# Forgetting attention in eight heads: row maxima as a running fused minimum, transposed by one matmul

## The chip, the cores and the metric

The kernel runs on one core of a Trainium2 chip. The time is the device time of one execution in microseconds (us). The engines are TensorE (PE; its weight loads are PEld), VectorE (DVE), ScalarE (ACT), GpSimd (POOL) and SyncE (SP, which here only issues transfers).

## The reference

One layer over a sequence of 2048 tokens with 1024 channels. A normalised input is projected into three groups of heads: a gated linear recurrence, a pooling mixer, and a causal attention of 8 heads of 64 channels with a forgetting term. The branches are gated, concatenated and projected back. The change touches the attention alone:

```python
c = jnp.cumsum(log_f, axis=1).transpose(0, 2, 1)
scale = D ** -0.5
for i in range(T // Q_BLOCK):
    s = jnp.einsum('bqhd,bkhd->bhqk', q[:, q0:q1], k[:, :q1]).astype(jnp.float32) * scale
    mask = (q0 + jnp.arange(Q_BLOCK))[:, None] >= jnp.arange(q1)[None, :]
    bias = jnp.where(mask, c[:, :, q0:q1, None] - c[:, :, None, :q1], 0.0)
    p = jax.nn.softmax(jnp.where(mask, s + bias, MASK_VALUE), axis=-1)
    outs.append(jnp.einsum('bhqk,bkhd->bqhd', p.astype(v.dtype), v[:, :q1]))
```

So each row of scores has q·k / 8 plus c at the query minus c at the key, and the softmax needs something near the row's maximum to be subtracted before the exponential.

## The kernel before

**Up to the attention.** Until about 673 us of the profiled execution the kernel normalises and projects, runs the recurrence (the tiles S, el and pu belong to it), and writes the attention's q and k as float16 pairs (high and low part) to scratch memory (qh_d, ql_d, kh_d, kl_d). `fgates` cumulates the forget gates; it leaves the cumulated gate of each key, scaled, as two rows per head in c_d (chi and clo, with rows of 256 ahead of them), the reference value of each query group in cref8, and the bias of the exponential in biasg. The pooling mixer (tile mb among others) comes next, and then v.

**The attention.** Queries are worked on in 4 groups (g) of 512 tokens, 8 heads (h) each, so 32 pairs of group and head; keys come in chunks (c) of 512. Group g sees chunks 0 to g. For each pair there are two passes.

- `max_steps` finds the row maxima. For each block of 128 queries (qi) and each chunk, PE makes the scores `mx` (512 keys wide; in the last, diagonal chunk 128 to 512) from QM and KA. Rows 0 to 63 of these are q and k; a few rows from 64 on carry the constants and the gate (68 rows in all). DVE reduces each mx to one value per query: a plain reduction (L979) for a whole chunk, and for the diagonal one a fused operation that adds the mask negq and takes the maximum (L976, two instructions in the trace: the operation and a read of its accumulator). Then L985 takes the maximum over the chunks, L986 adds cref8 and scales, and L988 and L989 split the result in a float16 pair, Mc. Three passes later (MTL), `mt` turns Mc with four matmuls (L995), one for each 128 queries, into two rows of 512, and ACT copies them to rows 64 and 65 of QB (L997). The helper `bank` gives the PSUM tiles: three for mx, two for st, one for o and two for ty, which mt, the gate projection and the output share.
- `scores` and `values` make the attention itself: for each 128 keys (j) two matmuls fill `st` (L1009 from the high and low parts, L1010 from KA and QB, where QB's maxima meet the 256s in KA), and on the diagonal a third adds the mask (L1012). ACT takes the exponential as float32 (pf, L1019) and as float16 (ph, L1023; every third one is made by POOL, L1021), and DVE or POOL subtracts the two (pl, L1024). `values` multiplies both with v in `o` (L1034 to L1036), and after a head's last key DVE divides (rl, oc).

**Order.** A list `deadlines` spreads the passes of `max_steps` over the steps of the head before (LEAD steps ahead of their use), and generators fill the remaining room: the gate projection (pgc), the loads of the output weights (wo, wol), then the output projection (y, yt, L1078 to L1095) of groups that are done. The order in which each engine gets its instructions is then set by a scheduler, and each engine runs its own in order.

Of the kernel before, what the change touches and what calls it, by code (L numbers as in the profile page):

```python
# [54 lines left out]
def kernel(  # L55
# [33 lines left out]
    cref8 = cp.tile([P, NG, 8], F32, tag="cref8", name="cref8")  # L89
# [8 lines left out]
    c_d = tc.dram_tile([4, 8, T], F16, name="c_d")  # L98
# [611 lines left out]
    def fgates():  # L710
# [53 lines left out]
        V.tensor_scalar(c32, crs[0], -1.0 / 32, None, op0=ALU.mult)  # L764
# [4 lines left out]
        for i, src in enumerate((c256, c256, chi, clo)):  # L769
            nc.sync.dma_start(c_d[i].rearrange("h (t c) -> t h c", c=P), src)  # L770
# [21 lines left out]
    def kload(c):  # L792
        tok = ds(c * GT, GT)
        nc.sync.dma_start(KA[c][64:68], c_d[:, :, tok])
        nc.sync.dma_start(KA[c][0:64], kh_d[:, :, tok].rearrange("c (e p) t -> p (c e) t", p=64))
        nc.sync.dma_start(K2[c][0:64], kh_d[:, :, tok].rearrange("c (e p) t -> p (c e) t", p=64))
        nc.sync.dma_start(K2[c][64:128], kl_d[:, :, tok].rearrange("c (e p) t -> p (c e) t", p=64))
# [158 lines left out]
    def max_steps():  # L956
        for n, (g, h) in enumerate(order):
# [7 lines left out]
            M = wk.tile([P, 4, 4], F32, tag="M", name=f"M{g}_{h}", bufs=2) if g else None  # L965
            Mf = wk.tile([P, 4], F32, tag="Mf", name=f"Mf{g}_{h}", bufs=2)
            left = MTL if n else 0
            for qi in range(4):
                for c in range(g + 1):
# [3 lines left out]
                    PE.matmul(mx[:, :w], QMs[i][:68, qi * P:(qi + 1) * P], KA[c][:68, h, :w], start=True, stop=True)  # L973
                    dst = M[:, qi, c:c + 1] if g else Mf[:, qi:qi + 1]
                    if last:
                        V.tensor_tensor_reduce(mx[:, :w], mx[:, :w], negq[:, GT - w:], 1.0, -3e38,  # L976
                                               op0=ALU.add, op1=ALU.max, accum_out=dst)
                    else:
                        V.tensor_reduce(dst, mx[:, :w], op=ALU.max, axis=AX.X)  # L979
# [4 lines left out]
            if g > 0:  # L984
                V.tensor_reduce(Mf, M[:, :, :g + 1], op=ALU.max, axis=AX.X)  # L985
            V.tensor_scalar(Mf, Mf, cref8[:, g, h:h + 1], -1.0 / 256, op0=ALU.add, op1=ALU.mult)  # L986
            Mc = wk.tile([P, 4, 2], F16, tag="Mc", name=f"Mc{g}_{h}", bufs=2)
            V.tensor_copy(Mc[:, :, 0], Mf)  # L988
            V.tensor_tensor(Mc[:, :, 1], Mf, Mc[:, :, 0], op=ALU.subtract)  # L989
            yield n  # L990

            def mt(g=g, h=h, i=i, Mc=Mc):
                pt = bank("ty", f"mt{g}_{h}")
                for qi in range(4):
                    PE.matmul(pt[64:66, qi * P:(qi + 1) * P], Mc[:, qi, :], idh, start=qi == 0, stop=qi == 3,  # L995
                              skip_group_check=True)
                S.activation(QBs[i][64:66], pt[64:66], AF.Copy, bias=0.0, scale=1.0)  # L997
# [4 lines left out]
    def scores(n, g, h, j):  # L1002
# [7 lines left out]
        PE.matmul(st[:, off:], KA[c][:68, h, jj * P:(jj + 1) * P], QBs[i][:68, off:], start=False, stop=not diag)  # L1010
# [192 lines left out]
```

## Time and profile before

| | us |
|---|---|
| runs: median of 3 (lowest to highest) | 1248.82 (1247.80 to 1250.89) |
| the profiled execution | 1248.18 |
| its span in the profile | 1246.4 |
| PE / DVE / ACT / POOL busy | 1170.5 / 812.2 / 609.5 / 403.7 |
| first row maximum, last row maximum (matmul mx) | 673.1, 1144.4 |

A row of a group of instructions reads: line of the kernel, engine, operation, output <- inputs, shape, count, then busy time in us and the mean length of one in ns, then idle time of the engine just ahead of them and what ended it. In a row of a tile, three numbers divided by strokes are the shortest, median and longest duration in ns. Granted clock is 0.987 on average. Matmuls are pipelined: one of 512 columns is listed with 0.38 us though the next starts after 0.22.

### The profile page before, as it was taken

The page shows a single profiled execution, that of the slowest core. Times are in us where ns is not written, and L with a number is a line of the kernel's source. Part 1 is how long each engine was busy: PE and PEld are TensorE (multiplying, and loading weights), DVE is VectorE, ACT ScalarE, POOL GpSimd, SP SyncE. Part 2 cuts the span into 40 slices and gives each one's busy share as a digit, 9 for nine tenths or more (in the row PEclk, how much of TensorE's full clock was granted, in tenths as well). Part 3 has the DMA queues.
Part 4 walks back from the last instruction along what each step waited for, and adds up shares of the span by engine and source line. Part 5 has one row for each costly group of instructions (what it writes and reads, how often), then busy time and mean ns, then how long its engine had stood idle before and what let it go on. Part 6 is the DMA issues. An engine that isn't in the chain of part 4 may idle for free.

```text
span 1246.4 us, 25487 instructions
## 1 busy us (share of the span) xinstructions
PE 1170.5 (94%) x9949; PEld 749.9 (60%) x9949; DVE 812.2 (65%) x1736; ACT 609.5 (49%) x1176; POOL 403.7 (32%) x500
## 2 busy tenths in 40 slices
PE   5877999999999999999999999999989899999998
PEld 3445667655644588884447767755555555555544
DVE  5787878887433243214364799788788888888522
ACT  5756444553121222212122677667767676777611
POOL 2645555553130020002230223234334343434400
PEclk9988999999999999999999999999999999999999
DMA  9646100113175232101112343285223222321263
GB/s 226 184 115 170 44 17 18 52 35 93 43 183 142 71 107 71 35 2 43 26 51 70 89 140 110 69 178 127 67 64 85 68 78 79 65 51 38 80 162 104
DMA packets 168137, 107.56 MB, mean 86 GB/s; under 512 B 95824, under 2 KB 159568, under 8 KB 168016
## 3 DMA queue, kind: packets, MB, share of 16 engines
q1 hardware_dynamic: 166976, 105.92, 32.2%
q8 instruction: 78, 1.28, 0.4%
q14 instruction: 43, 0.35, 0.1%
q10 hardware_dynamic: 1040, 0.00, 0.0%
HBM read 59.62 MB, written 31.59 MB: 73 GB/s over the span
## 4 chain that ended last, share of the span: by engine, by line
PE 62%; DVE 19%; ACT 6%; issue 5%; POOL 4%; DMA 4%; SPq 0%; POOLq 0%; DVEq 0%; ACTq 0%
PE y L1078 11%; PE pq L183 7%; PE pv L194 6%; PE pgc L194 5%; PE pu L183 3%; PE st L1009 3%; PE st L1010 3%; PE pgb L183 3%; PE pk L183 3%; DVE pl L1024 3%; PE mx L973 3%; DVE M L979 3%; PE o L1034 2%; PE o L1035 2%; PE pf L183 2%
## 5 line engine op out<-in xcount | busy, mean ns | idle before, releaser
L1019 ACT ACTIVATE pf<-st,biasg 128x512 f32<-128x512 f32 (+1 forms) x320 | 199.6, 625 | 93.9 <-PE st L1010 53.2
L194 PEld LDWEIGHTS <-hTh 128*128 128x128 f16 x1536 | 151.0, 99 | 44.3 <-DMA hTh<-xh 16.1
L1024 DVE TENSOR_TENSOR pl<-pf,ph 128x512 f16<-128x512 f32 (+1 forms) x213 | 139.9, 658 | 42.4 <-POOL ph L1021 24.8
L1024 POOL TENSOR_TENSOR pl<-pf,ph 128x512 f16<-128x512 f32 (+2 forms) x107 | 114.2, 1067 | 147.7 <-ACT ph L1023 137.6
L979 DVE TENSOR_REDUCE M<-mx 128x1 f32<-128x512 f32 x192 | 129.2, 682 | 9.4 <-PE mx L973 8.5
L1023 ACT ACTIVATE ph<-st,biasg 128x512 f16<-128x512 f32 (+2 forms) x213 | 131.4, 617 | 2.1 <-PE o L1036 2.1
L1034 PE MATMUL o<-Vt,ph 128*128 128x65 f16 x1088 | 129.7, 193 | 2.8 <-DVE oc L1048 2.4
L1035 PE MATMUL o<-Vt,ph 128*128 128x64 f16 x1088 | 130.2, 195 | 0.0
L1036 PE MATMUL o<-Vt,pl 128*128 128x65 f16 x1088 | 129.2, 192 | 0.0
L1021 POOL TENSOR_SCALAR ph<-pf 128x512 f16<-128x512 f32 (+1 forms) x107 | 66.0, 617 | 192.4 <-ACT pf L1019 130.8
L1034 PEld LDWEIGHTS <-ph 128*128 128x128 f16 x1088 | 102.6, 96 | 34.5 <-issue 5.5
L1009 PE MATMUL st<-QQ,K 128*128 128x512 f16 (+1 forms) x320 | 111.5, 349 | 5.6 <-ACT ph L1023 5.0
L1035 PEld LDWEIGHTS <-ph 128*128 128x128 f16 x1088 | 101.8, 97 | 24.5 <-issue 1.1
L1036 PEld LDWEIGHTS <-pl 128*128 128x128 f16 x1088 | 102.3, 99 | 0.4
L1078 PE MATMUL y<-woh,mh 128*128 128x512 f16 (+2 forms) x264 | 98.2, 373 | 0.0
L1078 PE MATMUL y<-woh,ml 128*128 128x512 f16 (+2 forms) x264 | 98.0, 373 | 0.0
L1078 PE MATMUL y<-wol,mh 128*128 128x512 f16 (+2 forms) x264 | 98.0, 373 | 0.0
L973 PE MATMUL mx<-KA,QM 68*128 68x512 f16 (+1 forms) x224 | 79.5, 358 | 5.7 <-DVE M L979 4.1
L194 PEld LDWEIGHTS <-hTl 128*128 128x128 f16 x768 | 75.5, 98 | 9.9
L1010 PE MATMUL st<-QB,KA 68*128 68x512 f16 x224 | 80.1, 358 | 0.0
L1078 PEld LDWEIGHTS <-mh 128*128 128x128 f16 x528 | 49.4, 98 | 50.4 <-issue 0.7
L976 DVE CUSTOM_DVE_ANT_0 mx<-mx,negq 128x128 f32<-128x128 f32 (+3 forms) x128 | 62.3, 492 | 12.0 <-PE mx L973 11.5
(327 smaller groups left out, 2691.1 us busy)
## 6 DMA issues: line engine op xcount, KB each, us to landing
xt<-in_x_dram SPq DMA_DIRECT2D x16, 512.0 KB, 4.4
xr<-in_x_dram SPq DMA_DIRECT2D x16, 512.0 KB, 4.5
out_dram<-yt SPq DMA_DIRECT2D x15, 512.0 KB, 3.1
QQ<-qh_d SPq DMA_DIRECT2D x64, 64.0 KB, 2.3
wo<-in_w_out_dram SPq DMA_DIRECT2D x16, 256.0 KB, 3.0
gc_d<-gtc SPq DMA_DIRECT2D x32, 128.0 KB, 2.0
gtl<-gc_d SPq DMA_DIRECT2D x16, 256.0 KB, 2.9
wst_q<-in_w_in_dram SPq DMA_DIRECT2D x12, 256.0 KB, 2.9
```

The costliest lines, as they stand in the source:

```text
L183: PE.matmul(ps, a[:, k, c0:c0 + P], b[:, k, :], start=i == 0, stop=i == 3 * KC - 1)
L194: PE.matmul(ps, a[:, k, :], b[:, k, c0:c0 + n], start=i == 0, stop=i == 3 * KC - 1)
L979: V.tensor_reduce(dst, mx[:, :w], op=ALU.max, axis=AX.X)
L1009: PE.matmul(st[:, off:], K2[c][:, h, jj * P:(jj + 1) * P], QQs[i][:, off:], start=True, stop=False)
L1010: PE.matmul(st[:, off:], KA[c][:68, h, jj * P:(jj + 1) * P], QBs[i][:68, off:], start=False, stop=not diag)
L1019: S.activation(pf[:, off:], st[:, off:], AF.Exp, bias=bias, scale=0.125)
L1023: S.activation(ph[:, off:], st[:, off:], AF.Exp, bias=bias, scale=0.125)
L1024: (G if k == 1 else V).tensor_tensor(pl[:, off:], pf[:, off:], ph[:, off:], op=ALU.subtract)
L1034: PE.matmul(pov[:, qi, :], ph[:, qs], Vt[:, j, h, 0:65], start=(j == 0 and qi == 0), stop=False, skip_group_check=True)
L1035: PE.matmul(pov[:, qi, 0:64], ph[:, qs], Vt[:, j, h, 65:129], start=False, stop=False, skip_group_check=True)
L1036: PE.matmul(pov[:, qi, :], pl[:, qs], Vt[:, j, h, 0:65], start=False, stop=(j == 4 * g + qi), skip_group_check=True)
L1078: PE.matmul(py, a[:, k, :], b[:, k, cs], start=i == 0, stop=i == 3 * KC - 1)
```

## The change

It keeps a running minimum of the negated maxima. The scores of a chunk are multiplied by -1/256 in the same fused operation that reduces them, with the value after the earlier chunks as the start of the minimum, so that the value after the last chunk is the result. For this the gate rows of c_d are now relative to each group's own reference, and `gap8`, made once in `fgates`, has the distance from group to group; it is added in the fused operation as a broadcast operand where the mask stands for the diagonal chunk. The reduction over chunks and the scaling go.

The four blocks of 128 queries of Mc are transposed by one matmul into eight rows, two for each block. DVE multiplies them with `bm`, a table of ones and zeros, into rows 64 to 71 of QB, so that each block's two rows are nonzero only in its own 128 columns. ACT's copy goes. KA and QM get ten rows from 64 on instead of four.

```diff
-        G.memset(qm[64:68], 256.0)
-        G.memset(qm[64:66], 0.0)
+        G.memset(qm[64:74], 256.0)
+        G.memset(qm[64:72], 0.0)
...
+    G.memset(bm, 1.0)
+    G.affine_select(out=bm, in_=bm, pattern=[[-2, 4]], compare_op=ALU.is_ge, fill=0.0, base=-64, channel_multiplier=1)
+    G.affine_select(out=bm, in_=bm, pattern=[[2, 4]], compare_op=ALU.is_ge, fill=0.0, base=65, channel_multiplier=-1)
...
+        for g in range(NG):
+            V.tensor_tensor(gap8[:, g], cref8[:, g:g + 1, :].to_broadcast([P, NG, 8]), cref8, op=ALU.subtract)
...
-        V.tensor_scalar(c32, crs[0], -1.0 / 32, None, op0=ALU.mult)
+        for g in range(NG):
+            V.tensor_scalar(c32[32 * g:32 * g + 32], crs[g][32 * g:32 * g + 32], -1.0 / 32, None, op0=ALU.mult)
...
-        for i, src in enumerate((c256, c256, chi, clo)):
+        for i, src in enumerate((c256,) * 8 + (chi, clo)):
             nc.sync.dma_start(c_d[i].rearrange("h (t c) -> t h c", c=P), src)
...
-        nc.sync.dma_start(KA[c][64:68], c_d[:, :, tok])
+        nc.sync.dma_start(KA[c][64:74], c_d[:, :, tok])
...
-                    PE.matmul(mx[:, :w], QMs[i][:68, qi * P:(qi + 1) * P], KA[c][:68, h, :w], start=True, stop=True)
-                    dst = M[:, qi, c:c + 1] if g else Mf[:, qi:qi + 1]
-                    if last:
-                        V.tensor_tensor_reduce(mx[:, :w], mx[:, :w], negq[:, GT - w:], 1.0, -3e38,
-                                               op0=ALU.add, op1=ALU.max, accum_out=dst)
-                    else:
-                        V.tensor_reduce(dst, mx[:, :w], op=ALU.max, axis=AX.X)
+                    PE.matmul(mx[:, :w], QMs[i][:74, qi * P:(qi + 1) * P], KA[c][:74, h, :w], start=True, stop=True)
+
+                    off = negq[:, GT - w:] if last else gap8[:, g, c, h:h + 1].to_broadcast([P, w])
+                    V.tensor_tensor_reduce(mx[:, :w], mx[:, :w], off, -1.0 / 256, M[:, qi, c - 1:c] if c else 3e38,
+                                           op0=ALU.add, op1=ALU.min, accum_out=M[:, qi, c:c + 1])
...
-            if g > 0:
-                V.tensor_reduce(Mf, M[:, :, :g + 1], op=ALU.max, axis=AX.X)
-            V.tensor_scalar(Mf, Mf, cref8[:, g, h:h + 1], -1.0 / 256, op0=ALU.add, op1=ALU.mult)
             Mc = wk.tile([P, 4, 2], F16, tag="Mc", name=f"Mc{g}_{h}", bufs=2)
-            V.tensor_copy(Mc[:, :, 0], Mf)
-            V.tensor_tensor(Mc[:, :, 1], Mf, Mc[:, :, 0], op=ALU.subtract)
+            V.tensor_copy(Mc[:, :, 0], M[:, :, g])
+            V.tensor_tensor(Mc[:, :, 1], M[:, :, g], Mc[:, :, 0], op=ALU.subtract)
...
-                for qi in range(4):
-                    PE.matmul(pt[64:66, qi * P:(qi + 1) * P], Mc[:, qi, :], idh, start=qi == 0, stop=qi == 3,
-                              skip_group_check=True)
-                S.activation(QBs[i][64:66], pt[64:66], AF.Copy, bias=0.0, scale=1.0)
+                PE.matmul(pt[64:72, :P], Mc.rearrange("p q two -> p (q two)"), idh, start=True, stop=True)
+                V.tensor_tensor(QBs[i][64:72].rearrange("p (q c) -> p q c", q=4),
+                                pt[64:72, :P].unsqueeze(1).to_broadcast([8, 4, P]),
+                                bm[64:72].unsqueeze(2).to_broadcast([8, 4, P]), op=ALU.mult)
...
-        PE.matmul(st[:, off:], KA[c][:68, h, jj * P:(jj + 1) * P], QBs[i][:68, off:], start=False, stop=not diag)
+        PE.matmul(st[:, off:], KA[c][:74, h, jj * P:(jj + 1) * P], QBs[i][:74, off:], start=False, stop=not diag)
```

The order of the instructions on the engines shows what moves. In these rows mx_5_3_2 is head 5, query block 3, chunk 2, pl_4_5 is head 4, key block 5, and the last number of a name is that of its buffer; ISA is the fused operation or, with one name only, the read of its accumulator. On DVE, in group 2 at the end of head 5, before:

```order
L976 ISA mx_5_3_2_11253,M_5_10947<-mx_5_3_2_11253,negq 128x512 [waits PE_49]
L976 ISA M_5_10947 128x1
L1051 TENSOR_TENSOR oc_2_10852<-oc_2_10852,gtl_2_10853 128x512 [waits DMAHW2_49,DVE_49]
L1024 TENSOR_TENSOR pl_4_5_11234<-pf_4_5_11232,ph_4_5_11233 128x512 [waits PE_49,Activation_49]
L985 TENSOR_REDUCE Mf_5_10948<-M_5_10947 128x4 [waits DVE_49]
L1024 TENSOR_TENSOR pl_4_6_11266<-pf_4_6_11264,ph_4_6_11265 128x512 [waits PE_49,Pool_49]
L411 TENSOR_TENSOR mx_2_l<-oc_2_10852,mx_2_h 128x512 [waits Activation_49]
L986 TENSOR_SCALAR Mf_5_10948<-Mf_5_10948,cref_74 128x4 [waits DVE_49]
L979 TENSOR_REDUCE M_6_11289<-mx_6_0_0_11291 128x1 [waits PE_49]
L988 CAST Mc_5_11258<-Mf_5_10948 128x4 [waits DVE_49]
L979 TENSOR_REDUCE M_6_11289<-mx_6_0_1_11315 128x1 [waits PE_49]
L989 TENSOR_TENSOR Mc_5_11258<-Mf_5_10948,Mc_5_11258 128x4 [waits DVE_49]
```

The same place of the changed kernel, on DVE:

```order
L987 ISA mx_5_3_2_11160,M_5_10858<-mx_5_3_2_11160,negq,M_5_10858 128x512 [waits DVE_49,PE_49]
L987 ISA M_5_10858 128x1
L1057 TENSOR_TENSOR oc_2_10765<-oc_2_10765,gtl_2_10766 128x512 [waits DMAHW0_49,DVE_49]
L1030 TENSOR_TENSOR pl_4_5_11141<-pf_4_5_11139,ph_4_5_11140 128x512 [waits PE_49,Activation_49]
L994 CAST Mc_5_11163<-M_5_10858 128x4 [waits DVE_49]
L1030 TENSOR_TENSOR pl_4_6_11171<-pf_4_6_11169,ph_4_6_11170 128x512 [waits PE_49,Pool_49]
L413 TENSOR_TENSOR mx_2_l<-oc_2_10765,mx_2_h 128x512 [waits Activation_49]
L995 TENSOR_TENSOR Mc_5_11163<-M_5_10858,Mc_5_11163 128x4 [waits DVE_49]
L987 ISA mx_6_0_0_11195,M_6_11194<-mx_6_0_0_11195,gap_74 128x512 [waits PE_49]
L987 ISA M_6_11194 128x1
L987 ISA mx_6_0_1_11219,M_6_11194<-mx_6_0_1_11219,gap_74,M_6_11194 128x512 [waits DVE_49,PE_49]
L987 ISA M_6_11194 128x1
```

The last step of Mc now stands ahead of the next head's first two maxima; before, it stood behind them. The second of these maxima takes the first one's result and waits for it on its own engine (DVE_49). Of the 192 fused operations with such an input, 52 stand directly behind the read that they need. On PE, at the transposition that follows, before:

```order
L973 MATMUL mx_6_0_2_11343<-K_9289,QM_3246 128x128 [waits DVE_49]
L995 LDWEIGHTS Mc_5_11258 [waits DVE_49]
L995 MATMUL mt_5_11346<-idh,Mc_5_11258 2x128
L995 LDWEIGHTS Mc_5_11258
L995 MATMUL mt_5_11346<-idh,Mc_5_11258 2x128
L995 LDWEIGHTS Mc_5_11258
L995 MATMUL mt_5_11346<-idh,Mc_5_11258 2x128
L995 LDWEIGHTS Mc_5_11258
L995 MATMUL mt_5_11346<-idh,Mc_5_11258 2x128
L1009 LDWEIGHTS K_9289
```

On PE, the changed kernel at the same place:

```order
L984 MATMUL mx_6_0_2_11247<-K_9232,QM_3247 128x128 [waits DVE_49]
L1000 LDWEIGHTS Mc_5_11163 [waits DVE_49]
L1000 MATMUL mt_5_11250<-idh,Mc_5_11163 8x128
L1015 LDWEIGHTS K_9232
L1015 MATMUL st_4_9_11253<-QQ_3240,K_9232 128x384 [waits Activation_49]
```

mt stays where it was, behind the third maximum of the next head, with one matmul instead of four. On DVE, shortly behind, the changed kernel has the write of QB that ACT had:

```order
L987 ISA mx_6_0_2_11247,M_6_11194<-mx_6_0_2_11247,negq,M_6_11194 128x128 [waits DVE_49,PE_49]
L987 ISA M_6_11194 128x1
L1030 TENSOR_TENSOR pl_4_8_11228<-pf_4_8_11226,ph_4_8_11227 128x512 [waits Activation_49]
L1001 TENSOR_TENSOR QB_3244<-mt_5_11250,bm 8x512 [waits PE_49]
L1030 TENSOR_TENSOR pl_4_9_11259<-pf_4_9_11257,ph_4_9_11258 128x384 [waits Pool_49]
```

It stands behind the reduction of the mx that PE makes just ahead of mt, with one pl between them.

More of the change, by code (lines that the diff above doesn't have):

```diff
@@ L88 @@
     biasg = cp.tile([P, NG, P], F32, tag="biasg", name="biasg")
-    cref8 = cp.tile([P, NG, 8], F32, tag="cref8", name="cref8")
+    gap8 = cp.tile([P, NG, NG, 8], F32, tag="gap8", name="gap8")
+    bm = cp.tile([P, 4], F32, tag="bm", name="bm")
     qh_d = tc.dram_tile([4, P, T], F16, name="qh_d")
@@ L97 @@
     gc_d = tc.dram_tile([T, 512], F32, name="gc_d")
-    c_d = tc.dram_tile([4, 8, T], F16, name="c_d")
+    c_d = tc.dram_tile([10, 8, T], F16, name="c_d")
     mh_d = tc.dram_tile([T, 6 * P], F16, name="mh_d")
@@ L698 @@
         qm = vp.tile([P, GT], F16, tag=f"QM{i}", name=f"QM{i}")
-        G.memset(qm[64:68], 256.0)
-        G.memset(qm[64:66], 0.0)
+        G.memset(qm[64:74], 256.0)
+        G.memset(qm[64:72], 0.0)
         qb = vp.tile([P, GT], F16, tag=f"QB{i}", name=f"QB{i}")
-        G.memset(qb[64:68], 0.0)
+        G.memset(qb[64:74], 0.0)
         QMs.append(qm)
@@ L756, in fgates @@
         V.tensor_copy(dl, pdl[:, :NG])
+        cref8 = fp.tile([P, NG, 8], F32, tag="cref8", name="cref8")
         V.tensor_scalar(cref8.rearrange("p g h -> p (g h)"), pcr[:, :32], 8.0, None, op0=ALU.mult)
+        for g in range(NG):
+            V.tensor_tensor(gap8[:, g], cref8[:, g:g + 1, :].to_broadcast([P, NG, 8]), cref8, op=ALU.subtract)
         crs = []
@@ L964, in max_steps @@
             nc.sync.dma_start(QBs[i][0:64], ql_d[h // 2, r, tok])
-            M = wk.tile([P, 4, 4], F32, tag="M", name=f"M{g}_{h}", bufs=2) if g else None
-            Mf = wk.tile([P, 4], F32, tag="Mf", name=f"Mf{g}_{h}", bufs=2)
+            M = wk.tile([P, 4, NG], F32, tag="M", name=f"M{g}_{h}", bufs=2)
             left = MTL if n else 0
```

## The prediction

> **What bounds the kernel now.** I read the page first, then busy time by stage, then the waits, the groups and the order of time on VectorE (DVE), the engine that gets the new work. The page: the span, the two busiest engines, and the chain of waits by engine.
>
> ```profile
> span 1246.4 us, 25487 instructions
> PE 1170.5 (94%) x9949; PEld 749.9 (60%) x9949; DVE 812.2 (65%) x1736; ACT 609.5 (49%) x1176; POOL 403.7 (32%) x500
> PE 62%; DVE 19%; ACT 6%; issue 5%; POOL 4%; DMA 4%; SPq 0%; POOLq 0%; DVEq 0%; ACTq 0%
> ```
>
> TensorE (PE) is the bound over the whole, DVE comes second. The change lies in the attention, where these shares differ. The next rows are stretches: everything from 343 us up to the first row maximum, then the four query groups as the row maxima reach them (from 673.1, 716, 824 and 994 us), then the tail. Columns: stretch, length, busy time of each engine.
>
> ```profile
> core 0: us, PE busy (x) PEld busy (x) DVE busy (x) ACT busy (x) POOL busy (x), PEclk, DMA share, GB/s
> 343.00:673.00 330.00, 325.33 (x2170) 214.10 (x2169) 116.10 (x250) 75.63 (x173) 49.57 (x66) 1.00 0.27 73
> 673.10:716.00 42.90, 41.05 (x447) 31.21 (x445) 32.33 (x120) 25.20 (x53) 9.05 (x14) 0.96 0.27 77
> 716.00:824.00 108.00, 102.65 (x1228) 77.55 (x1225) 92.56 (x242) 75.59 (x149) 33.32 (x42) 1.00 0.39 107
> 824.00:994.00 170.00, 157.10 (x1793) 92.71 (x1792) 147.93 (x330) 118.89 (x218) 65.81 (x78) 1.00 0.41 100
> 994.00:1148.00 154.00, 148.50 (x1681) 86.84 (x1680) 133.59 (x275) 112.64 (x199) 62.78 (x73) 0.99 0.25 63
> ```
>
> From 673 to 1148 us, 475 us in all, DVE is busy 32.3 + 92.6 + 147.9 + 133.6 = 406 us (86%) and PE 449 us (95%, its ends modelled). DVE has some 69 us of slack, so it is not idle cover: PE and DVE are near each other. ScalarE (ACT), at 332 us (70%), has room. The chain inside this stretch, by line:
>
> ```profile
> by line: PE y L1078 13.1%; PE pgc L194 9.5%; PE st L1009 7.8%; DVE pl L1024 7.5%; PE mx L973 7.4%; PE st L1010 7.3%; DVE M L979 7.0%; PE o L1034 4.5%; PE o L1035 4.5%; PE o L1036 4.3%; issue 3.4%; DVE mx L976 2.8%; DMA wo<-in_w_out_dram 2.1
> ```
>
> The plain reductions (L979) stand on it with 7.0% of 475 us, 33 us. Their group, with the others of DVE in the same stretch:
>
> ```profile
> L1024 DVE TENSOR_TENSOR pl<-pf,ph 128x512 f16<-128x512 f32 (+1 forms) x198 | 130.6, 661 | 30.4 <-POOL ph L1021 20.6 <-ACT ph L1023 7.9
> L979 DVE TENSOR_REDUCE M<-mx 128x1 f32<-128x512 f32 x192 | 129.2, 682 | 9.4 <-PE mx L973 8.5
> L976 DVE DVE_READ_ACCUMULATOR2_ANT M<- 128x1 f32 x96 | 13.3, 139 | 0.0
> L1086 DVE TENSOR_TENSOR yt<-y,gpo 128x512 f32<-128x512 f32 x17 | 11.6, 683 | 0.6 <-ACT ojunk L1085 0.4
> L986 DVE TENSOR_SCALAR Mf<-Mf,cref 128x4 f32<-128x4 f32 x32 | 10.4, 327 | 0.3
> L985 DVE TENSOR_REDUCE Mf<-M 128x4 f32<-128x8 f32 (+2 forms) x24 | 3.8, 157 | 0.2
> ```
>
> 33 of 129.2 us: a microsecond of DVE work costs 0.26 us of time today. The subtraction pl (L1024) gives the same, 7.5% of 475 = 36 of 130.6 us, 0.27. Who waits for whom in the stretch (total, times, longest):
>
> ```profile
> ACT QB L997 <- PE mt L995: 12.8, 14, 3.8
> DVE mx L976 <- PE mx L973: 11.5, 21, 1.8
> PE mx L973 <- DVE M L979: 6.1, 8, 1.8
> PE mt L995 <- DVE Mc L989: 5.9, 7, 1.2
> PE mx L973 <- DVE M L976: 2.5, 3, 2.0
> ```
>
> PE stands 8.6 us for a bank of row scores that DVE has not reduced, and 5.9 us for Mc, the two-part maxima that the transposing matmul mt takes. DVE stands for PE as well. Two engines wait for each other in turn.
>
> **The change, part by part.** *The reduction.* 192 plain reductions become the fused operation plus a read of its accumulator; the 128 diagonal ones have that already. DVE in order of time (start, length):
>
> ```profile
> 1028.45 0.68 DVE L979 TENSOR_REDUCE M<-mx 128x1 f32<-128x512 f32 x1
> 1029.06 0.69 DVE L976 CUSTOM_DVE_ANT_0 mx<-mx,negq 128x512 f32<-128x512 f32 x1
> 1029.66 0.14 DVE L976 DVE_READ_ACCUMULATOR2_ANT M<- 128x1 f32 x1
> 1029.84 0.17 DVE L985 TENSOR_REDUCE Mf<-M 128x4 f32<-128x16 f32 x1
> ...
> 865.48 0.14 DVE L976 DVE_READ_ACCUMULATOR2_ANT M<- 128x1 f32 x1
> 865.48 0.69 DVE L1024 TENSOR_TENSOR pl<-pf,ph 128x512 f16<-128x512 f32 x1
> ```
>
> From start to start the reduction takes 0.61 us (1028.45 to 1029.06) and the fused one 0.60 (1029.06 to 1029.66). The read costs nothing where the next instruction does not need it (both at 865.48), and 0.18 us where it does (1029.66 to 1029.84). So the swap as such is nearly free. What is new is that 192 of the 320 now take the maximum so far as a per-partition operand. No such fused operation is in the trace; the nearest row with a per-partition operand beside a PSUM tensor and an SBUF tensor is mb, against 683 ns of yt, which has none:
>
> ```profile
> L867 DVE SCALAR_TENSOR_TENSOR mb<-pp,pscl,gtb x8: 742/746/750, 581.5 to 654.2; 128x512 f32<-128x512 f32 x8
> L378 DVE SCALAR_TENSOR_TENSOR S<-S,el,pu x64: 254/280/289, 74.8 to 326.6; 64x64 f32<-64x64 f32 x64
> ```
>
> 0.746 - 0.683 = 0.06 us, times 192 = 12 us. In the order of the changed kernel 52 of the 192 stand directly behind the read that they need: 52 x 0.18 = 9 us. Together 21 us of DVE; the ends are 0 (operand free, PE late anyway) and 192 x 0.24 = 46 us (each one exposed). I take 21, since mb has the operands and the order has the neighbours.
>
> *The bookkeeping.* The reduction over chunks (L985, 3.8 us) and the scaling (L986, 10.4) go: -14.2 us of DVE. The two steps that make Mc stay.
>
> *The transposition.* Four matmuls a head become one: 96 go. Around one of them:
>
> ```profile
> 929.92 0.22 PE L973 MATMUL mx<-K,QM 68*128 68x128 f16 x1
> 931.33 0.38 PE L995 MATMUL mt<-idh,Mc 128*2 128x128 f16 x4 [1.18 <-DVE Mc L989]
> ```
>
> Four take 0.38 us where one takes 0.22, so each further one starts 0.053 later: 96 x 0.053 = 5 us of PE, at most, and I count it all, PE being the chain for most of the time. This row also shows the wait. DVE, at the same place:
>
> ```profile
> 929.05 0.22 DVE L986 TENSOR_SCALAR Mf<-Mf,cref 128x4 f32<-128x4 f32 x1
> 929.19 0.68 DVE L979 TENSOR_REDUCE M<-mx 128x1 f32<-128x512 f32 x1
> 929.79 0.83 DVE L988 CAST Mc<-Mf 128x4 f16<-128x4 f32 x1
> 930.53 0.68 DVE L979 TENSOR_REDUCE M<-mx 128x1 f32<-128x512 f32 x1
> 931.13 0.15 DVE L989 TENSOR_TENSOR Mc<-Mf,Mc 128x4 f16<-128x4 f32 x1
> ```
>
> Two reductions of the next head stand between the steps. In the new order both steps of Mc stand ahead of them, some 1.2 us earlier, as long as these seven waits. But a DVE that is behind is late for something else next, a bank of mx above all: of 5.9 us I count 3 as saved, between 0 and 5.9.
>
> *The write of QB* moves from ACT to DVE:
>
> ```profile
> L997 ACT ACTIVATE QB<-mt 2x512 f16<-2x512 f32 x32 | 18.8, 588 | 14.2 <-PE mt L995 13.5
> ```
>
> On ACT it lay off the path, and I count nothing for its going. On DVE it is a product of 8 x 512 read from PSUM. By yt it takes 0.683 us; the 8 partitions save nothing, as S with 64 partitions and 64 elements takes 280 ns. 32 x 0.683 = 22 us (19 if each overlaps the next as the reductions do). Behind it in DVE's queue stand pl and the next maxima, for which PE waits. It waits for mt, as ACT did; since PE issues mt just behind the mx whose reduction stands ahead of QB, I count no stall. The consumer, the second score matmul, follows some passes later.
>
> One rule of the Trainium skill speaks against this part: VectorE: DVE Perf Modes, section "Two Vector instructions with no wait between them", says that an instruction whose operands start in another quadrant of partitions than those of the one before starts only when all earlier ones have finished. QB starts at partition 64, so it and its successor would each lose the 0.08 us by which 0.68-us operations overlap here: 64 x 0.08 = 5 us more of DVE, an estimate that by the price below makes the sum 2 us longer.
>
> *Before the attention*: six more stores of c_d, ten rows instead of four into KA, four products for gap8, four partial scalings, wider memsets. PE is busy 325.3 of 330 us there and DVE 116, so these have cover: 0, at most +1 us. The matmuls contract 74 rows instead of 68: nothing, as 68 and 128 rows take the same:
>
> ```profile
> L1009 PE MATMUL st<-QQ,K 128*128 128x512 f16 x224 | 85.1, 380 | 4.5 <-ACT ph L1023 4.1
> L1010 PE MATMUL st<-QB,KA 68*128 68x512 f16 x176 | 67.0, 381 | 0.0
> ```
>
> *The sum.* DVE: +21 + 22 - 14 = +29 us, which takes it from 406 to 435 of 475 us (86 to 92%) beside a PE that gets lighter. The price of 0.27 is that of today; as DVE's slack shrinks from 69 to 40 us, the price rises towards 1. I take 0.42, nearer the row: 29 x 0.42 = +12. PE -5, the wait for Mc -3. Together +4 us, on the profiled execution's 1248.2: 1252.2. It stands 0.6 us below the median of the runs shown (1248.82), so 1252.8, rounded 1253. Ends: DVE +29 - 21 + 3 for a free operand and shorter QB would be near +5, at 0.27 +1, with -5 and -6: -10, 1239; DVE +54 at 0.6, +32, with -5: +27, 1276.
>
> **The rivals.** About 0.3% (3.7 us) is what a measurement of this kernel can tell from no change.
>
> *Faster: DVE's load stays in its slack* (0.28). For it: 69 us of slack, of which 20 us are waits for PE's own mx, and seven waits for Mc that the order undoes. Then the exposed reads cost nothing (+12 + 19 - 14 = +17 of DVE, at 0.27 +5), PE -5, Mc -6: -6 us, 1243. It decides itself at PE's wait for mx: if that stays near 9 us, this holds. Against it: those waits come in turn, and a longer pass on DVE moves the next one.
>
> *No change* (0.29): the same 29 us at today's price, +8, against -5 and -3: 1249.
>
> *DVE becomes the bound* (0.07, within slower): with 435 us of work and the last group at 134 + 15 of 154 us, the price is near 1: +29 - 5 - 3 = +21, 1270. Against it: three banks of mx and five of pl still let the engines slip past each other.
>
> *The running maximum contends with GpSimd* (0.03, within slower): its operands in SBUF are two. L1024, with two SBUF inputs, shows such stalls:
>
> ```profile
> L1024 DVE TENSOR_TENSOR pl<-pf,ph x213: 274/681/1667, 680.4 to 1175.3; 128x512 f16<-128x512 f32 x75, 128x384 f16<-128x384 f32 x15, 128x128 f16<-128x128 f32 x9, 128x256 f16<-128x256 f32 x8
> ```
>
> Were the 192 held up by 0.1 us on average, that is +19 of DVE, +8 us: 1261. Against it stands S, with a per-partition operand and a tensor in SBUF: 254 to 289 ns, never stalled. The Trainium skill, SBUF — State Buffer, section "Who interferes with whom", has the contention for two SBUF inputs and doesn't say whether a per-partition operand is one; by S it is none.
>
> *The change doesn't do what it says* (0.01): excluded but for numbers of the schedule, since the new order shows one mt a head and the fused pairs.
>
> **How the numbers follow.** Slower 0.43 (my sum, 1253, in its own range 1250 to 1262, with the two heavier cases), same 0.29, faster 0.28. The range reaches from 1240 (faster, near its end) to 1266, leaving out DVE as a full bound and the last of the gains.
>
> **What would show it.** Fused operations with the running maximum near 0.75 us; DVE busy near 435 us from the first row maximum to the last; mt with 32 records and a wait for Mc under 3 us; QB on DVE near 0.68 us; PE's wait for mx grown from 9 towards 20 us. If that wait stays, the forecast is wrong towards faster. If QB waits long for mt, or fused operations take over 0.85 us, it is wrong towards slower.

## The result, and the profile after

| | before | after |
|---|---|---|
| median of 5 runs (lowest to highest), us | 1250.89 (1247.80 to 1251.91) | 1256.60 (1254.60 to 1258.87) |
| the profiled execution, us | 1248.18 | 1254.60 |

The ratio is 1.0052, with a 95% interval from 1.0037 to 1.0067: the change made the kernel slower by some 6 us. The prediction was 1253, with slower as its likeliest case.

The page of the changed kernel, with the same three lines as before:

```profile
span 1252.9 us, 25621 instructions
PE 1170.2 (93%) x9853; PEld 749.3 (60%) x9853; DVE 846.7 (68%) x1911; ACT 589.9 (47%) x1144; POOL 414.0 (33%) x503
PE 63%; DVE 18%; issue 6%; ACT 5%; POOL 4%; DMA 4%; SPq 0%; DVEq 0%; POOLq 0%; ACTq 0%
```

96 matmuls are gone (9949 to 9853), and still PE is listed as busy for the same time. DVE has 34.5 us more in all. The stretches again, each from a group's first row maximum to the next group's. Of before stand here the last three, since the prediction began its last group at 994 us where group 3 begins at 962.7, and the sum from the first to the last row maximum:

```profile
716.00:822.50 106.50, 101.35 (x1221) 77.01 (x1218) 91.06 (x238) 74.09 (x147) 32.57 (x41) 1.00 0.38 106
822.50:962.70 140.20, 131.03 (x1485) 76.93 (x1482) 122.07 (x277) 99.79 (x182) 55.06 (x66) 1.00 0.44 104
962.70:1144.40 181.70, 172.26 (x1968) 101.12 (x1965) 157.92 (x327) 129.81 (x232) 71.96 (x85) 0.99 0.25 64
673.10:1144.40 471.30, 445.69 (x5104) 286.27 (x5102) 403.38 (x958) 328.88 (x611) 168.65 (x204) 0.99 0.34 87
```

And of after:

```profile
343.00:672.10 329.10, 325.39 (x2171) 214.12 (x2170) 117.34 (x257) 75.63 (x173) 49.42 (x66) 1.00 0.29 75
672.10:711.70 39.60, 38.29 (x426) 29.50 (x424) 34.34 (x121) 21.51 (x46) 10.11 (x15) 1.00 0.30 83
711.70:820.30 108.60, 100.36 (x1197) 76.10 (x1194) 98.28 (x259) 68.56 (x137) 32.10 (x41) 1.00 0.37 104
820.30:967.10 146.80, 136.28 (x1463) 80.16 (x1459) 134.18 (x335) 95.29 (x174) 59.83 (x66) 0.94 0.42 100
967.10:1150.90 183.80, 172.61 (x1943) 100.56 (x1940) 168.96 (x414) 124.92 (x224) 75.11 (x86) 0.99 0.23 64
672.10:1150.90 478.80, 447.54 (x5011) 286.32 (x5009) 435.75 (x1126) 310.28 (x580) 177.16 (x205) 0.98 0.33 86
```

Until the attention nothing is lost: the first row maximum comes 1 us earlier. Group 0 is 3.3 us shorter, group 2 is 6.6 us longer, groups 1 and 3 are 2.1 us longer each, and from the first to the last row maximum it is 7.5 us. DVE is busy for 435.75 us from the first to the last row maximum, against 403.38. In group 2 the granted clock falls to 0.94. Who waits for whom in the attention (total, times, longest), and the groups of DVE:

```profile
PE o L1040 <- DVE oc L1054: 11.9, 10, 2.3
PE mx L984 <- DVE M L987: 9.4, 11, 2.2
PE mt L1000 <- DVE Mc L995: 2.7, 4, 1.9
L987 DVE CUSTOM_DVE_ANT_0 mx<-mx,gap,M 128x512 f32<-128x512 f32 x96 | 72.3, 753 | 7.2 <-PE mx L984 3.3
L987 DVE CUSTOM_DVE_ANT_0 mx<-mx,gap 128x512 f32<-128x512 f32 x96 | 67.2, 701 | 3.0 <-PE mx L984 2.4
L987 DVE DVE_READ_ACCUMULATOR2_ANT M<- 128x1 f32 x320 | 44.2, 138 | 0.3
L1001 DVE TENSOR_TENSOR QB<-mt,bm 8x512 f16<-8x512 f32 x32 | 22.1, 689 | 1.1 <-PE mt L1000 0.2
```

PE's wait for a bank of mx has hardly grown (8.6 us before). The wait that has grown is for o, which has one bank: PE may begin the next head's values only when DVE has divided the last head's (oc), and DVE comes to that late. Before, this row read:

```profile
PE o L1034 <- DVE oc L1048: 2.4, 6, 0.7
```

### The profile page after: what moved, and what is told of

Same layout as the page of the kernel before. It is cut to its first block, busy times and chain, and to the rows that moved or that the text cites. A ratio compares the mean times of both kernels' runs of the same rounds, so it can differ in the third digit from the quotient of the medians.

```text
span 1252.9 us, 25621 instructions
## 1 busy us (share of the span) xinstructions
PE 1170.2 (93%) x9853; PEld 749.3 (60%) x9853; DVE 846.7 (68%) x1911; ACT 589.9 (47%) x1144; POOL 414.0 (33%) x503
## 4 chain that ended last, share of the span: by engine, by line
PE 63%; DVE 18%; issue 6%; ACT 5%; POOL 4%; DMA 4%; SPq 0%; DVEq 0%; POOLq 0%; ACTq 0%
PE y L1084 11%; PE pq L185 7%; PE pv L196 6%; PE pgc L196 5%; DVE mx L987 4%; PE st L1015 4%; PE st L1016 3%; PE mx L984 3%; PE pu L185 3%; PE pgb L185 3%; PE pk L185 3%; PE o L1040 2%; PE o L1041 2%; PE o L1042 2%; DVE pl L1030 2%
## 5 line engine op out<-in xcount | busy, mean ns | idle before, releaser
L1030 POOL TENSOR_TENSOR pl<-pf,ph 128x512 f16<-128x512 f32 (+2 forms) x107 | 117.8, 1100 | 153.3 <-ACT ph L1029 144.9
L1040 PE MATMUL o<-Vt,ph 128*128 128x65 f16 x1088 | 132.1, 195 | 12.3 <-DVE oc L1054 11.9
L1040 PEld LDWEIGHTS <-ph 128*128 128x128 f16 x1088 | 104.2, 98 | 45.5 <-issue 15.2
L1027 POOL TENSOR_SCALAR ph<-pf 128x512 f16<-128x512 f32 (+1 forms) x107 | 69.5, 650 | 183.3 <-ACT pf L1025 124.8
L1041 PEld LDWEIGHTS <-ph 128*128 128x128 f16 x1088 | 103.4, 98 | 24.0 <-issue 1.6
L984 PE MATMUL mx<-KA,QM 74*128 74x512 f16 (+1 forms) x224 | 80.4, 363 | 3.4 <-DVE M L987 2.7
L1016 PE MATMUL st<-QB,KA 74*128 74x512 f16 x224 | 81.2, 363 | 0.1
L987 DVE CUSTOM_DVE_ANT_0 mx<-mx,gap,M 128x512 f32<-128x512 f32 x96 | 72.3, 753 | 7.2 <-PE mx L984 3.3
L987 DVE CUSTOM_DVE_ANT_0 mx<-mx,gap 128x512 f32<-128x512 f32 x96 | 67.2, 701 | 3.0 <-PE mx L984 2.4
```

Of the source, the lines that this page charges most:

```text
L987: V.tensor_tensor_reduce(mx[:, :w], mx[:, :w], off, -1.0 / 256, M[:, qi, c - 1:c] if c else 3e38, op0=ALU.add, op1=ALU.min, accum_out=M[:, ...
L1016: PE.matmul(st[:, off:], KA[c][:74, h, jj * P:(jj + 1) * P], QBs[i][:74, off:], start=False, stop=not diag)
L1030: (G if k == 1 else V).tensor_tensor(pl[:, off:], pf[:, off:], ph[:, off:], op=ALU.subtract)
L1040: PE.matmul(pov[:, qi, :], ph[:, qs], Vt[:, j, h, 0:65], start=(j == 0 and qi == 0), stop=False, skip_group_check=True)
L1041: PE.matmul(pov[:, qi, 0:64], ph[:, qs], Vt[:, j, h, 65:129], start=False, stop=False, skip_group_check=True)
```

## The experiments

Each ran in five rounds beside the kernel before on one chip, in four sessions on different chips, so kernels are compared by their ratios to before. "Running value" is the value that a fused operation starts from.

**First: which half of the change, and is it VectorE's total?** The rivals were the prediction's (DVE's load at 0.42 us per us) and the clock, which falls behind long waits of PE.

`mt_only`: before with the transposition by one matmul and the eight rows written by DVE; the maxima as before.

```diff
 (before)
-                for qi in range(4):
-                    PE.matmul(pt[64:66, qi * P:(qi + 1) * P], Mc[:, qi, :], idh, start=qi == 0, ...)
-                S.activation(QBs[i][64:66], pt[64:66], AF.Copy, bias=0.0, scale=1.0)
+                PE.matmul(pt[64:72, :P], Mc.rearrange("p q two -> p (q two)"), idh, start=True, stop=True)
+                V.tensor_tensor(QBs[i][64:72]..., pt[64:72, :P]..., bm[64:72]..., op=ALU.mult)
```

> The transposition alone (one matmul into eight rows, the product into QB on VectorE, ten constant rows), with the reductions, the maximum over chunks and the scaling as before. Theory load (the loss is VectorE's added work at some 0.4 us of time for each us): +22 us of VectorE is +9, -5 of TensorE, -1 of waiting: +2 to +4 us on before, ratio 1.002 to 1.003. Theory clock (the loss is the granted clock, halved behind waits of TensorE of 1.9 us and more): ratio 1.000 unless the half-clock time between 660 and 1200 us of the span grows past some 7 us; each us of it costs 0.5 us. Theory order (the scheduler's other order costs it, whatever the load): no prediction, any sign within 0.4%.

1248.05 us, ratio 0.9976 (0.9966 to 0.9986), below what the theories of load and clock gave. The transposition as a whole is a gain of 3 us, though DVE is busy for 16 us longer (first to last row maximum 419.4 us), and though PE's clock is halved for 13.6 us of the attention, twice as long as before.

`run_only`: the running value alone, with four transposing matmuls, ACT's copy and four constant rows as before.

```diff
 (after)
-                PE.matmul(pt[64:72, :P], Mc.rearrange("p q two -> p (q two)"), idh, start=True, stop=True)
-                V.tensor_tensor(QBs[i][64:72]..., op=ALU.mult)
+                for qi in range(4):
+                    PE.matmul(pt[64:66, qi * P:(qi + 1) * P], Mc[:, qi, :], idh, start=qi == 0, ...)
+                S.activation(QBs[i][64:66], pt[64:66], AF.Copy, bias=0.0, scale=1.0)
```

> The running fused minimum alone (with gap8 and the gate rows relative to each group), transposed by four matmuls and copied by ScalarE as before. Theory load: fused operations with the running value at 753 instead of 682 ns and their reads, less the 14 us of bookkeeping, is some +13 us of VectorE: +5, less 3 of waiting for Mc: +2 us, ratio 1.001 to 1.002, so that this and the transposition alone together give about the loss of the whole change. Theory clock: the ratio follows the half-clock time in the attention, 0.5 us for each us over 7.

1257.40 us, 1.0053 (1.0033 to 1.0072): all of the loss, where the load theory gave 1.001 to 1.002, though DVE is busy for only 414.7 us, less than in `mt_only`. PE's waits have moved in the same manner as in the whole change:

```profile
PE mx L984 <- DVE M L987: 9.3, 11, 2.2
PE o L1040 <- DVE oc L1054: 8.4, 6, 2.3
```

`qb_act`: the whole change, with the eight rows written by four ACT operations in place of DVE's product.

```diff
 (after)
-                V.tensor_tensor(QBs[i][64:72]..., pt[64:72, :P]..., bm[64:72]..., op=ALU.mult)
+                for qi in range(4):
+                    S.activation(QBs[i][64:72, qi * P:(qi + 1) * P], pt[64:72, :P], AF.Copy, bias=0.0, scale=bm[64:72, qi:qi + 1])
```

> The whole change, but the eight rows go to QB by four operations of ScalarE (128 columns each, with the table of ones and zeros as scale) instead of one product on VectorE. Theory load: -22 us of VectorE at 0.4 is -9 on the changed kernel, and ScalarE gets 128 x 0.3 = 38 us, of which it had 20 before: ratio to before 0.997 to 0.999, faster than the changed kernel by 5 to 9 us. Theory clock: the same, if the waits over 1.9 us go; else the changed kernel's 1.005 stays. Rival: ScalarE is late with the exponentials, and it is 1.005 or more.

1255.73 us, 1.0044 (1.0029 to 1.0060): taking 22 us from DVE brings nothing that can be told from the whole change's 1.0052.

`no_chain`: the whole change, but every fused operation starts afresh at 3e38, and the minimum over the chunks is taken by 24 small reductions.

```diff
 (after)
-                    V.tensor_tensor_reduce(mx[:, :w], mx[:, :w], off, -1.0 / 256, M[:, qi, c - 1:c] if c else 3e38,
+                    V.tensor_tensor_reduce(mx[:, :w], mx[:, :w], off, -1.0 / 256, 3e38,
...
+                V.tensor_reduce(Mf, M[:, :, :g + 1], op=ALU.min, axis=AX.X)
```

> The whole change, but each fused operation starts its minimum afresh and a reduction over the chunks (24 of them, in groups 1 to 3) stands ahead of Mc, as before. The fused operations should be 0.69 us again instead of 0.75. Theory load: -12 us of VectorE for the operand, -5 for reads waited for, +4 for the reductions: -13 x 0.4 = -5 us on the changed kernel: ratio to before 1.000 to 1.003. Theory clock: by the half-clock time in the attention. If the chain's waits cost nothing and the operand is hidden, 1.005 stays.

1247.28 us, 0.9976 (0.9963 to 0.9988), less than any of the theories gave. The gain of `mt_only` is back, with DVE busy for 424.3 us. So the fused operations, their scaling and gap8 cost next to nothing; what costs is that a value is handed from one to the next. DVE's total does not rank these four kernels: `qb_act` (413.1 us) and `run_only` have the least of it and are slow.

**Second: the operand, or the wait for it?** A running value is two things: an operand from a tile (753 against 701 ns above) and a dependency on the instruction ahead.

`const_operand`: `no_chain`, with a constant column in place of the immediate.

```diff
 (no_chain)
-                    V.tensor_tensor_reduce(mx[:, :w], mx[:, :w], off, -1.0 / 256, 3e38,
+                    V.tensor_tensor_reduce(mx[:, :w], mx[:, :w], off, -1.0 / 256, idf[:, 64:65] if c else 3e38,
```

> The whole change, but the fused operations from the second chunk on start from a constant per-partition operand (a column of 3e38) in place of the value that the operation ahead has just read out, and the minimum over the chunks is taken by 24 small reductions as in the kernel no_chain (0.9976 of before). The operand is there, the dependency is gone. If the 60 ns that an operand from a tile adds to a fused operation is what costs (theory operand): 192 x 0.06 = 11.5 us more of VectorE than in no_chain, and a ratio of 1.004 to 1.006, as the whole change has. If it is the wait for the value just read (theory dependency): the fused operations still take 0.75 us, but the ratio stays by no_chain's, 0.996 to 1.000.

1249.85 us, 0.9997 (0.9986 to 1.0007), by the upper end of what the dependency theory said. The fused operations take 751 ns, as in the whole change:

```profile
L988 DVE CUSTOM_DVE_ANT_0 mx<-mx,gap,idf 128x512 f32<-128x512 f32 x96 | 71.3, 751 | 1.7 <-PE mx L985 1.4
```

So the operand costs 0.0021, or 2.6 us, against `no_chain` (by the ends of the two intervals between -0.0002 and 0.0044, so it may be nothing), and the dependency is the rest: 0.0055, 6.9 us, against the whole change (0.0030 to 0.0081). The order of time on DVE shows it. First the whole change, then `const_operand`, at the same place (start, length):

```profile
1006.99 0.14 DVE L987 DVE_READ_ACCUMULATOR2_ANT M<- 128x1 f32 x1
1007.27 0.76 DVE L987 CUSTOM_DVE_ANT_0 mx<-mx,gap,M 128x512 f32<-128x512 f32 x1
```

```profile
1004.33 0.14 DVE L988 DVE_READ_ACCUMULATOR2_ANT M<- 128x1 f32 x1
1004.33 0.75 DVE L988 CUSTOM_DVE_ANT_0 mx<-mx,gap,idf 128x512 f32<-128x512 f32 x1
```

The operation that needs the read starts 0.28 us after the read began; the one that doesn't starts with it. Over the trace of the whole change 52 fused operations stand directly behind the read that they need, and start 0.285 us after it began in the median; in `const_operand` 58 stand directly behind a read, with a median of 0.

`c_outer`: the whole change with the chunks as the outer loop, so that the value was read four passes earlier.

```diff
 (after)
-            for qi in range(4):
-                for c in range(g + 1):
+            for c in range(g + 1):
+                for qi in range(4):
```

> The whole change with its running value and operand, but the loop over the chunks stands outside that over the four query blocks, so that the value that a fused operation starts from was read out four passes earlier. Theory operand: the same 192 operands, a ratio of 1.004 to 1.006. Theory dependency: no operation waits any more for the read right ahead of it, so 0.996 to 1.000. The other order of the diagonal chunk (its four short passes now stand side by side at a head's end) may move it by 0.002 either way.

1253.46 us, 1.0025 (1.0013 to 1.0036): between the two theories. The loops also move the diagonal's short passes, so this needed a control, `c_outer_const`: the same order with the constant operand.

```diff
 (const_operand)
-            for qi in range(4):
-                for c in range(g + 1):
+            for c in range(g + 1):
+                for qi in range(4):
```

> The kernel const_operand (0.9997) with the loop over the chunks outside that over the query blocks, as in c_outer (1.0025): the order of c_outer, the operand, no value handed on. If the order alone makes c_outer slower than const_operand (theory order): 1.002 to 1.004. If it is the value handed on, even four passes later (theory dependency): 0.999 to 1.001.

1254.61 us, 1.0038 (1.0024 to 1.0053). In this order the kernel is as slow without a running value as with it. A value handed on from four passes back thus costs nothing that shows, and the order costs some 0.004 by itself. The miss of `c_outer` was an experiment that changed two things.

**Third: what is a microsecond of DVE worth?** One more operation a head that nobody reads, in three kernels.

```diff
 (after: dve_more; no_chain: fresh_more; before: before_more, over the two rows and behind ACT's copy)
+                V.tensor_reduce(idf[64:72, 0:4], pt[64:72, :P].unsqueeze(1).to_broadcast([8, 4, P]), op=ALU.max, axis=AX.X)
```

> The whole change with one more VectorE operation of about 0.69 us a head that nobody reads, right behind the one that writes the eight rows: some 22 us more of VectorE. At the prediction's price of 0.42 us per us of VectorE, 9 us: a ratio of 1.012. If work of that kind lies in VectorE's slack, as the run with the rows written by ScalarE suggests, 1.005 to 1.008.

> The kernel before with one more VectorE operation of about 0.69 us a head that nobody reads, behind the copy of the transposed maxima: some 22 us more of VectorE. At 0.42 us per us: 1.007. If work of that kind lies in VectorE's slack at before's load: 0.999 to 1.003.

> The kernel no_chain (fresh start of every fused operation, minimum by 24 reductions; 0.9976 of before) with the same extra VectorE operation of about 0.69 us a head that made the whole change 11.5 us slower and the kernel before 2 us slower. VectorE then carries some 22 us more than in no_chain and more than in the whole change, with no value handed on. If a microsecond of VectorE simply costs more the less of it is idle (theory load): as at the whole change's load, 0.4 to 0.53 us a microsecond, 9 to 12 us, a ratio of 1.005 to 1.007. If it costs that much only where a fused operation waits for the one ahead of it (theory dependency): as in before_more, 2 to 4 us, 0.999 to 1.001.

| kernel | DVE busy, first to last row maximum | ratio (interval) | the addition costs | per us of DVE |
|---|---|---|---|---|
| `before_more` | 403.4 to 422.1 | 1.0014 (1.0004 to 1.0024) | 0.0014, 1.8 us | 0.08 |
| `fresh_more` | 424.3 to 441.4 | 1.0040 (1.0025 to 1.0055) | 0.0064, 8.0 us | 0.36 |
| `dve_more` | 435.8 to 455.4 | 1.0146 (1.0126 to 1.0167) | 0.0094, 11.7 us | 0.53 |

The last column divides by 32 x 0.69 = 22 us; with the intervals each price is good to about 0.1 to 0.15. It is the price of an operation at this place, which also keeps mt's PSUM bank in use for longer, in all three kernels, and it has in it what PE's clock lost (in `dve_more` the median clock is 0.9795, in the whole change 0.983). `dve_more` came out above both of its expectations. The price is not a constant: nearly nothing at the load of before, a third to a half past some 425 us. `fresh_more`, with nothing handed on, came out nearer to the load theory than to the dependency theory, so load does cost, late.

`mt_act`: `mt_only` with the four ACT operations of `qb_act` in place of DVE's product.

```diff
 (mt_only)
-                V.tensor_tensor(QBs[i][64:72]..., pt[64:72, :P]..., bm[64:72]..., op=ALU.mult)
+                for qi in range(4):
+                    S.activation(QBs[i][64:72, qi * P:(qi + 1) * P], pt[64:72, :P], AF.Copy, bias=0.0, scale=bm[64:72, qi:qi + 1])
```

> The kernel mt_only (one matmul for the transposition, the eight rows written by VectorE; 0.9976) with the eight rows written by four ScalarE operations. It tells what that exchange costs without the running value: VectorE has 22 us less, ScalarE some 30 us more. If ScalarE's part is hidden and VectorE's is worth 0.08 us a microsecond: 0.996 to 0.998. If ScalarE's part costs as much as VectorE's relief brings in the whole change (where the exchange moved the time by under 0.1%), it costs more here, where VectorE has slack: 0.999 to 1.004.

1249.85 us, 0.9996 (0.9984 to 1.0008): four short ACT operations a head cost 0.0020 against `mt_only`, 2.5 us, though ACT is far from full; by the ends of the two intervals it is between -0.0002 and 0.0042. That may be a part of why `qb_act` gained nothing from a lighter DVE.

**Last: take the wait away and leave the rest.** `pairs`: the whole change, with two query blocks taken in turn, so that between a read and the operation that needs it stands the other block's.

```diff
 (after)
-            for qi in range(4):
-                for c in range(g + 1):
+            for qi, c in [(q0 + e, c) for q0 in (0, 2) for c in range(g + 1) for e in range(2)]:
```

> The whole change, with two query blocks taken in turn: their passes over a chunk stand side by side, so that a fused operation starts from the value read out two fused operations earlier. Everything else of the change stays, the second semaphore of these operations too. In the whole change a fused operation right behind the read it needs starts 0.284 us after that read began, against 0 us with a constant operand, some 55 times: 15.6 us of VectorE. If those waits are a part of VectorE's load and the load sets the time (theory load): VectorE occupied for 453 to 463 us in place of 469, and 0.998 to 1.002. If it is the running value with its second semaphore wherever it stands (theory second semaphore): 1.004 to 1.006. If the places of the short diagonal passes cost (theory order): as in the kernel with the chunks outermost, 1.002 to 1.004 with the waits gone.

1248.15 us, 0.9983 (0.9974 to 0.9993): faster than before, and 0.0069 (8.6 us) below the whole change; by the ends of the two intervals between 0.0044 and 0.0093. Running value, operand, second semaphore and the sum of DVE's busy time are all there still; from 672 to 1155 us it is 441.1 us here and 439.8 in the whole change. What has gone stands in the order of time on DVE:

```profile
1005.77 0.75 DVE L987 CUSTOM_DVE_ANT_0 mx<-mx,gap,M 128x512 f32<-128x512 f32 x1
1006.44 0.14 DVE L987 DVE_READ_ACCUMULATOR2_ANT M<- 128x1 f32 x1
1006.44 0.76 DVE L987 CUSTOM_DVE_ANT_0 mx<-mx,gap,M 128x512 f32<-128x512 f32 x1
```

The second of these takes the other block's value and starts with the read at 1006.44. Group 3 shrinks from 183.8 to 177.9 us and group 2 from 146.8 to 144.3, with a clock of 0.96 there in place of 0.94:

```profile
823.40:967.70 144.30, 133.85 (x1461) 78.62 (x1458) 135.06 (x333) 95.19 (x174) 60.01 (x66) 0.96 0.43 102
967.70:1145.60 177.90, 168.92 (x1908) 98.63 (x1905) 166.13 (x411) 124.33 (x223) 73.72 (x85) 1.00 0.24 66
```

`pairs` moves the diagonal's short passes a little too, and `c_outer` showed that this can matter. But `const_operand` took the wait away with the loops of the whole change and gave back 6.9 us: two ways, each with something else changed beside it, and both put most of the loss on the wait for the read right ahead. How the wait reaches PE is less clear. The longer wait for o is a part of it at most, since `pairs` keeps most of that wait and is faster than before:

```profile
PE mx L984 <- DVE M L987: 9.1, 15, 2.2
PE o L1040 <- DVE oc L1054: 8.4, 9, 1.9
```

Three versions beat both kernels, and cannot be told from each other: `mt_only` (0.9976), `no_chain` (0.9976) and `pairs` (0.9983).

**What stays open.** `run_only` and `qb_act` are as slow as the whole change although DVE is busy for 21 to 23 us less in them. That the waits cost at any load fits both, and the 51 and 49 waits are in their traces, but why they cost as much there as at the higher load was not tried apart. The clock has a share. Of the six executions of `run_only`, two took 1252.2 and 1253.2 us at granted clocks of 0.986 and 0.987, and four 1257.1 to 1258.5 at 0.980 to 0.982. Within the kernels, 0.001 of mean clock goes with 0.6 us. The whole change has 0.983 in the median and the kernel before 0.986, so some 2 of the 6 us came by that way. `run_only` has 0.982, also some 2 us, and `qb_act` 0.979, some 4 us of its 5.5: in that kernel most of the loss goes with the clock, and what lowered the clock was not tried.

## Why the prediction was right, and where its steps were not

The direction, the load and the total came out; two terms of the sum were mis-sized in opposite directions, and their errors nearly cancelled. That the total came so near is luck: with either term alone put right, the forecast would have been about 1246 or 1257 us.

- *Reduction, the operand* (0.06 us each, 12 us of DVE): measured 753 against 701 ns, 0.052. In time 2.6 us (perhaps nothing), where 12 x 0.42 gave 5. The contention with GpSimd, a rival, did not occur. The row shows 723 to 759 ns for all 96 whole-chunk operations with the operand, where pl ranged up to 1667 ns:

```profile
L987 DVE CUSTOM_DVE_ANT_0 mx<-mx,gap,M x96: 723/755/759, 824.3 to 1151.8; 128x512 f32<-128x512 f32 x96
```

- *Reduction, the exposed reads* (52 x 0.18 = 9 us of DVE, at 0.42 worth 4 us): the count was right, 52. Each is 0.285 us, not 0.18: the row it came from has a small reduction behind the read, not a fused operation. That makes 15 us of DVE, 6 us at 0.42. Measured are 8.6 us (`pairs`) or 6.9 (`const_operand`), a price of 0.58 or 0.47. So the term was too small by some half, in part by the length and in part by the price.
- *Bookkeeping* (-14.2 us of DVE): gone as forecast. Against it stand the operands and the switch to fused operations; from `mt_only` to `pairs`, which differ in all of these, the time moves by 0.0007, within the intervals.
- *Transposition* (PE -5) and *write of QB* (+22 us of DVE at 0.42, +9): together +4 in the sum, -3.0 measured (`mt_only`, which is the transposition without the running value; -1.8 to -4.3). The matmul is there as said, and QB at 689 ns for 683. What failed is the price: at the load of before a microsecond of DVE costs 0.08 (`before_more`), less than the chain's 0.27; a row's share of the chain did not say how much of an addition would be hidden. With 0.08 the sum is 22 x 0.08 - 5 = -3.2, as measured; the -5 itself was not measured apart.
- *The wait for Mc* (-3): 5.9 to 2.7 us. Right as a wait; what it saved in time was not measured apart.
- *Before the attention, 74 rows*: nothing, as forecast (PE 325.4 us in both).
- *DVE busy near 435 us*: 435.75, in part by luck: it rose by 32 us from 403.4, where the prediction had 29 from 406, a sum that ran to 1148 us and not to the last row maximum. The price, one number for all terms, was the weak point: it depends on the load.
- *The lower end of the range*: it is written as 29 - 21 + 3, but its 5 us are 29 - 21 - 3, which is what a shorter QB means; the end itself stands.
- *The sign to look for*: PE's wait for mx was to grow from 9 towards 20 us, and "if that wait stays, the forecast is wrong towards faster". It stayed at 9.4 and the kernel was slower, so the sign failed: the wait that grew was the one for oc and the single bank of o (2.4 to 11.9 us), which the prediction did not look at. That it carries the loss is not shown, since `pairs` has 8.4 us of it.
- *The rule of the Trainium skill* (VectorE: DVE Perf Modes, section "Two Vector instructions with no wait between them"): it held. Where the operation ahead of QB takes 0.69 us, as QB does, the next one starts 0.72 us after each of them. The last two rows show an operation of that length away from QB, where the next one starts after 0.61 us:

```profile
933.26 0.69 DVE L1030 TENSOR_TENSOR pl<-pf,ph 128x512 f16<-128x512 f32 x1
933.98 0.69 DVE L1001 TENSOR_TENSOR QB<-mt,bm 8x512 f16<-8x512 f32 x1
934.70 0.56 DVE L1030 TENSOR_TENSOR pl<-pf,ph 128x384 f16<-128x384 f32 x1
...
1007.94 0.69 DVE L1030 TENSOR_TENSOR pl<-pf,ph 128x512 f16<-128x512 f32 x1
1008.55 0.75 DVE L987 CUSTOM_DVE_ANT_0 mx<-mx,gap,M 128x512 f32<-128x512 f32 x1
```

`dve_more` points to the partition and not to QB as such. Its added operation idf also starts at partition 64; where it stands right behind QB (20 of 32 times) it starts 0.61 us after it, and the operation behind idf, back at partition 0, starts after 0.71 though idf is as long:

```profile
941.92 0.69 DVE L1001 TENSOR_TENSOR QB<-mt,bm 8x512 f16<-8x512 f32 x1
942.53 0.68 DVE L1004 TENSOR_REDUCE idf<-mt 8x4 f32<-8x512 f32 x1
943.24 0.56 DVE L1031 TENSOR_TENSOR pl<-pf,ph 128x384 f16<-128x384 f32 x1
```

64 x 0.11 = 7 us of DVE, for 5 estimated. What that cost in time was not measured apart; `mt_only`, where QB stands in the same manner, is faster than before.

- *The borders of the stretches*: group 3 starts at 962.7 us before the change, not at 994, so "the last group at 134 of 154 us" was a part of it. The whole group has DVE busy for 157.9 of 181.7 us, the same share.

## What to carry to other kernels

When a fused operation starts from what the one ahead of it has just read out, put another operation between the two: the same work in another order gave back 8.6 us. Price an added microsecond on a second engine by adding one and measuring, and at the load that the change leaves, since here it cost 0.08, 0.36 or 0.53 us. Look at every wait for the engine that gets the new work, not only at the one that leads the list today: here the wait for mx stayed and the wait for the one bank of o grew.

## What the hardware showed that was not expected

- A read of the accumulator is free (0 us from its start to the next operation's) unless the next operation needs it: then the next one starts 0.285 us after it (a fused operation) or 0.18 us (the small reduction of the kernel before). QB, with its other partitions, starts 0.17 us after one too. The Trainium skill, VectorE: DVE Perf Modes, section "The DRAIN you can't avoid", has it that a semaphore after each of eight copies cost nothing extra. Its case is copies; for this pair, of a read and the operation that needs its value, the trace shows a cost, and the measurement decides.
- PE's clock fell at waits of about 2 us. The whole change has six waits of PE between 1.8 and 2.3 us in the attention, and at five of them a window of half clock begins. One of these waits, and a stretch of 9 us around it:

```profile
824.20 0.27 PE L1000 MATMUL mt<-idh,Mc 128*8 128x128 f16 x1 [1.90 <-DVE Mc L995]
822.00:831.00 9.00, 7.07 (x72) 4.86 (x70) 8.81 (x25) 4.26 (x10) 2.68 (x4) 0.62 1.15 232
```

The granted clock is 0.62 over these 9 us: half speed for 6.8 of them. The length of the wait is not the whole rule. The sixth wait of the whole change, 2.09 us long, had no such window behind it, and in `mt_only` one begins at a wait of 0.61 us:

```profile
773.71 0.19 PE L1040 MATMUL o<-Vt,ph 128*128 128x65 f16 x1 [2.09 <-DVE oc L1054]
773.70:777.10 3.40, 3.39 (x65) 3.11 (x66) 3.11 (x6) 1.42 (x4) 0.24 (x1) 1.00 0.16 47
...
825.02 0.27 PE L999 MATMUL mt<-idh,Mc 128*8 128x128 f16 x1 [0.61 <-DVE Mc L994]
825.00:828.40 3.40, 3.38 (x40) 2.80 (x41) 3.31 (x9) 1.90 (x5) 0.71 (x1) 0.50 1.28 164
```

Windows of half clock come to 20.5 us of the attention in the whole change, 6.8 before, and 13.6 in `mt_only` and `pairs`, which are faster than before. `run_only`'s profile has 6.8 us as before and still takes 2.5 us longer from the first to the last row maximum (473.8 for 471.3). So the clock is a part of the loss and does not explain it alone.
